# Attention in a one-core hybrid block: fp32r transposes of two probability row blocks, read from a DMA copy

## The chip, the cores and the metric

The kernel runs on one core of one Trainium2 chip. The metric is the device time of one execution in microseconds (us), as the median over several executions. A profile is one further execution taken by the hardware profiler; its trace tells when each instruction of each engine started and ended. The engines are TensorE (PE for matmuls, PEld for the loads of their weights), VectorE (DVE), ScalarE (ACT), GpSimd (POOL) and SyncE (SP), which issues nearly all DMAs here.

## The reference

One decoder block over 1024 tokens of width 1024, in float32. The part that matters is the forgetting attention, 8 heads of dimension 64, causal:

```python
logits = jnp.einsum('bqhd,bkhd->bhqk', qi, k).astype(jnp.float32) * scale
logits = logits + ci[..., None] - c_k          # c: running sum of the log forget gates
logits = jnp.where(causal, logits, -jnp.inf)
p = jax.nn.softmax(logits, axis=-1).astype(v.dtype)
return jnp.einsum('bhqk,bkhd->bqhd', p, v)
```

Beside it stand a gated MLP branch (GELU, a norm by groups, a 128x128 spatial mix), an output projection with residual, and a ConvFFN (up projection to 5632, causal depthwise convolution of width 3, SiLU gate, down projection), each behind an RMSNorm, and a final RMSNorm.

## The kernel before

**Numbers.** Most matmuls run in fp32r, a 4-byte type that TensorE streams faster than float32. A float32 operand is split in a high part rounded to fp32r and the rest, and a product is made of three matmuls. The transposes of the probabilities are float32.

**Stages.** Input projections (to about 205 us of the trace), the eight heads with the output projection of the gated branch as filler work (to about 358 us), the attention's output projection, the up projection with the convolution, and the down projection.

**One head.** Queries are cut in eight row blocks of 128, j = 0 to 7. Row block j sees the keys up to its own, 128(j+1) columns. Its steps are:
- `logits_mm` (L1002): the logits of block j on TensorE, in PSUM.
- `logits_min` (L1014): DVE adds the mask, takes the row minimum of the negated logits and writes them to SBUF. The blocks are kept in pairs i = j // 2 in tiles with the tags of `TTAG` (L954): pair 3 (blocks 6 and 7, 896 and 1024 columns) stands in `t3` for even heads and in a tile of the tag `H` for odd ones; pair 2 in `t2` and `H`. `places[h, i]` names the two parts.
- `logits_exp` (L1037): ACT takes the exponential in place, with the row sums beside it.
- `turn_p` (L1057): TensorE turns 128x128 blocks of probabilities with an identity (L1064), up to four into one PSUM bank. ACT copies the bank to fp32r (L1065) and DVE the rest (L1066). The block that is turned is the matmul's weights; the identity streams.
- `values` (L1071): TensorE multiplies by V and accumulates over the key blocks.

**The order of a head.** `GROUPS` (L1045) lists nine groups of key blocks. For the query blocks 4 to 7 (half 1) key blocks 0 to 4 are a group each and turn four blocks; ((1,5),(1,7)) turns blocks 5, 6, 7 and 7; ((1,6),(0,2)) turns 6, 7 and two of the lower half; the rest are of the lower half. `STEPS` takes them two by two: five steps (s = 0 to 4) a head. In step n the loop (L1186) turns the groups of step n+1, then multiplies those of step n with logits of the next head between them: `NEXT` (L1152) gives blocks 7 and 6 in step 0, 5 and 4 in step 1, and so on. The exponentials of a step's logits follow one step later. So blocks 7 and 6 of head h+1 have their logits in step 0 of head h, their exponentials in step 1, and are first turned in step 4. `FILLS` puts twelve filler matmuls (`sg_out`, L1092, with a load of `xtok` and a store to `hpd`) into steps 2 and 4 of heads 1 to 5 and into some more before; heads 6 and 7 have none. `seq` (L781) ties all matmuls of the heads on TensorE in one written order.

**Queues.** Instructions without such a tie are put in order on their engine when the program is built, by when their inputs are thought to be ready. SP holds, among others: the loads of a head's queries and keys two heads ahead (`head_loads`, L888), the load of the turned row sums (`row_tail`, L956, L964), the loads of the attention's output weights into the tag `raw` (`wo_load`, L1125, L1128), which POOL splits (L1136, L1137), and behind them, into the same four `raw` buffers, the first loads of the up projection's weights (L1273, L1326). ACT, DVE and POOL work on each other's outputs and wait on semaphores.

**The identity** is made by POOL in float32 (L135, L136). It is also used for the turns of the gated branch (L843), the row sums (L961), the next stage's input (L1390) and two small ones (L512, L628).

**Tags** (`BUFS`, L97): `H` has four buffers of 8 KB a partition. They hold parts of the input and its combinations early on (L195, L196, L398), then the odd heads' row blocks and `attF`, the heads' outputs.

Of the kernel before, what the change touches and what calls it, by code (L numbers as in the profile page):

```python
# [8 lines left out]
F32 = mybir.dt.float32  # L9
F32R = mybir.dt.float32r  # L10
# [4 lines left out]
P = 128  # L15
# [59 lines left out]
def block_kernel(ctx: ExitStack, tc: tile.TileContext, xT, xtok, wuv, wuh, wv0, wva, wvk, wvl, wqk, cpk, bfv,  # L75
                 ggain, g2r, gfr, wsp, woa, wos, wup, wdn, out):
    nc = tc.nc
# [15 lines left out]
    def nm(s):  # L93
        uid[0] += 1
        return f"{s}_{uid[0]}"

    BUFS = {"x1": 4, "x2": 2, "t3": 1, "t2": 1, "t01": 1, "V": 4, "H": 4, "wy": 2, "gg": 2,  # L97
            "pt": 3, "G": 4, "A": 2, "whl": 4, "raw": 4}

    LATE = ("A", "G", "whl", "pt")  # L100
# [1 line left out]
    def sb(tag, shape, dt=F32):  # L102
        return (base if tag == "x1" else raws if tag == "raw" else late if tag in LATE else early).tile(shape, dt, tag=tag, bufs=BUFS[tag], name=nm(tag))

# [3 lines left out]
    def fbank():  # L108
        return psa.tile([P, 512], F32, tag=FTAG, bufs=FB, name=nm("pf"))
# [22 lines left out]
        pe.matmul(wps, warm[:, 0:P], warm, start=True, stop=True)  # L132
    dve.memset(one, 1.0)
    dve.memset(lim, BIG)
    ident = cst.tile([P, P], F32, name="ident")  # L135
    make_identity(nc, ident)  # L136
    maskb = cst.tile([P, P], BF16, name="maskb")
    pool.memset(maskb, 0.0)
    pool.affine_select(out=maskb, in_=maskb, pattern=[[-1, P]], compare_op=ALU.is_ge,
# [44 lines left out]
    def xset(tags):  # L184
        r = []
        for t in tags:
            if t == "x1":
                r.append([sb(t, [P, 2, 512], F32R) for _ in range(2)])
            else:
                b = sb(t, [P, 2, 2, 512], F32R)  # L190
                r.append([b[:, 0], b[:, 1]])
        return r

    RAW = {n: [sb(t, [P, 2, 512]) for t in tags] for n, tags in (
        ("x21", ("V", "V")), ("x11", ("H", "H")), ("x22", ("x1", "x2")), ("x12", ("t3", "t2")))}  # L195
    XS = {n: xset(tags) for n, tags in (("B11", ("V", "V")), ("T2", ("H", "H")), ("B21", ("x1", "x2")))}  # L196

    def xs(n, hl, k):
        return XS[n][k // 2][hl][:, k % 2, :]
# [581 lines left out]
    def seq(m):  # L781

        if order:
            after(tc, m, order[0])
        order[:] = [m]
# [165 lines left out]
    attF = [None] * 4  # L951


    TTAG = [("gg", "gg"), ("wy", "wy"), ("t2", "H"), ("t3", "H")]  # L954
    exs = []
    def row_tail(h):  # L956

        p, hh, rs = h // 2, h % 2, rows[h]
# [55 lines left out]
    def logits_min(h, j, ps):  # L1014

        i, jj = j // 2, j % 2
        w1, w2 = (2 * i + 1) * P, (2 * i + 2) * P
        if jj == 1:
            tp = sb(TTAG[i][h % 2], [P, w1 + w2])
            places[h, i] = (tp[:, 0:w1], tp[:, w1:w1 + w2])  # L1020
        n = (j + 1) * P
        mn = sml.tile([P, 1], F32, tag="mn", name=nm("mn"))
        o, s, k = places[h, i][jj], ps[:, 0:n], msk[:, 1024 - n:1024]
        if chunk(n) < min(n, 512):
            o, k = (v.rearrange("p (b c) -> p b c", b=2) for v in (o, k))
            s = ps.rearrange("p (b c) -> p b c", b=2)[:, :, 0:chunk(n)]
        m = dve.tensor_tensor_reduce(out=o, in0=s, in1=k, scale=ss1[:, j:j + 1],
                                     scalar=lim[:, 0:1], op0=ALU.add, op1=ALU.min, accum_out=mn)
        if h and j == 5:
            after(tc, m, recips[h - 1])  # L1030
        if h and j == 3:
            after(tc, m, los[-1])
        if h == 7 and j == 0:
            after(tc, m, los[-2])
        return mn

    def logits_exp(h, j, mn):  # L1037
        t = places[h, j // 2][j % 2]
# [18 lines left out]
    def turn_p(g):  # L1057

        ptr = bank()
        pt = sb("pt", [P, 2, 512], F32R)  # L1060
        for half, k, j0, c, w in spans(g):
            for j in range(j0, 4 * half + 4):
                o = c + (j - j0) * P
                seq(pe.transpose(ptr[:, o:o + P], places[g[0], j // 2][j % 2][:, k * P:(k + 1) * P], ident))  # L1064
        casts.append(act.copy(pt[:, 0, :], ptr))  # L1065
        los.append(dve.tensor_tensor(out=pt[:, 1, :], in0=ptr, in1=f32(pt[:, 0, :]), op=ALU.subtract))  # L1066
        return pt
# [24 lines left out]
    def sg_out(whs):  # L1092
        for hf in range(2):
            o = slice(hf * 512, hf * 512 + 512)
            for tt in range(8):
                if hf == 0 and tt == 6:
                    nxt = sg_load(1)
                ts_ = slice(tt * P, (tt + 1) * P)
                hs = sb("raw", [P, 512])
                sp.dma_start(out=hs, in_=xtok[ts_, o])  # L1100
                ps = fbank()
                for k in range(4):
                    w = whs[k]
                    seq(pe.matmul(ps, sgT[k][:, 0, ts_], w[:, 0, :], start=(k == 0), stop=False))  # L1104
                    seq(pe.matmul(ps, sgT[k][:, 0, ts_], w[:, 1, :], start=False, stop=False))
                    seq(pe.matmul(ps, sgT[k][:, 1, ts_], w[:, 0, :], start=False, stop=(k == 3)))
                def evac(ps=ps, hs=hs, tt=tt, o=o):
                    dve.tensor_tensor(out=hs, in0=ps, in1=hs, op=ALU.add)
                    sp.dma_start(out=hpd[tt, :, o], in_=hs)

                if dve.on:
                    EVAC.append(evac)
                else:
                    evac()
                if hf == 0 and tt == 7:
                    whs = [None] * 4
                    SPLIT[:] = [(whs, k, nxt[k]) for k in range(4)]
                yield
# [67 lines left out]
    for n, step in enumerate(STEPS):  # L1186
        h, s = n // 5, n % 5
        if s == 0 and h < 6:
            head_loads(h + 2)
        if h == 7 and s == 0:  # L1190
            for _ in filler:
                pass
            wo_load((0, 1))
            wo_load((2, 3))
        if h in (2, 4, 6) and s == 4:
            for o in (slice(0, 512), slice(512, 1024)):
                pair_half(h // 2 - 1, o)
        now, turned = turned, []
        last, due = due, []
        if n == 35:  # L1200
            psl.release()
            psl = tc.alloc_tile_pool(name="psc", bufs=4, space=bass.MemoryType.PSUM, reuse_waits="tile")
            banks8[0, 0] = lbank()
            wmm(0, 0, banks8[0, 0], (0,))
        for g in STEPS[n + 1] if n + 1 < len(STEPS) else []:
            if n == 36 and turned:
                for e in held + [mrow]:
                    after(tc, logits_exp(*e), casts[-1])
            turned.append(turn_p(g))
            if n == 36 and len(turned) == 2:  # L1210
                after(tc, casts[-1], exs[-1])
        if n == 34:
            mrow = (7, 0, logits_min(7, 0, mrow))
        if n == 33:

            held, last = last, []
        if n == 34:
            last, held = held[:1], held[1:] + last
        if n == 35:
            last, held = held[:1], held[1:]  # L1220
        if s == 1 and h % 2 == 0:
            attF[h // 2] = sb("H", [P, 2, 1024])
        if s == (1 if h < 7 else 2):
            recips[h] = dve.reciprocal(rows[h], rows[h])
        out_copy = None
        if n == 37:
            row_tail(7)
        if n in EARLY:
            wmm(0, 0, banks8[0, 0], EARLY[n])
        if n == 39:  # L1230
            banks8[4, 0] = lbank()
            wmm(4, 0, banks8[4, 0], (0,))
        for c, (g, pt, js) in enumerate(zip(step, now, NEXT[s])):
            out_copy = values(g, pt) or out_copy
            last_copy = out_copy
            if h < 7:
                for j in js:
                    if n == 33 and j == 0:
                        mrow = logits_mm(7, 0, place())
                        continue  # L1240
                    due.append((h + 1, j, logits_min(h + 1, j, logits_mm(h + 1, j, place()))))
            if s == 1 and h < 7 and c == 0:
                row_tail(h)

        for e in last:
            x = logits_exp(*e)
            after(tc, x, casts[-1] if n == 34 else out_copy or casts[-1])
        fill((h, s))
        for _ in range(min(len(SPLIT), 1 if n == 9 else 2)):
            ws_, k, wr = SPLIT.pop(0)  # L1250
            wt = sb("whl", [P, 2, 512], F32R)
            ws_[k] = wt
            after(tc, act.copy(wt[:, 0], wr), out_copy or casts[-1])
            pool.tensor_tensor(out=wt[:, 1], in0=wr, in1=f32(wt[:, 0]), op=ALU.subtract)
        if n == 2:
            vh = sb("A", [P, 2, 4, 256])
            sp.dma_start(out=vh, in_=vu.rearrange("h p m c -> p h m c"))
        if n in UPPER:
            tt = UPPER.index(n)
            low = evac_v(tt, 1, vh[:, tt // 4, tt % 4, :])  # L1260
            after(tc, low(), los[-1])
            after(tc, vhigh[0], exs[-1])
# [631 lines left out]
```

## Time and profile before

| | before |
|---|---|
| median of 3 executions | 1045.37 us (1044.67 to 1045.62) |
| profiled execution | 1043.81 us, its span 1042.1 us |
| granted TensorE clock, mean | 0.998 of full |
| matmuls on PE | 4998 |
| transposes of probabilities (L1064) | 288 |
| bytes by DMA | 161.66 MB, 155 GB/s over the span |

The span runs from the first to the last instruction. A line of a view names source line, engine, operation and the tiles written and read, out<-in, with the buffer's tag (`t` for `t3`, `H`, `gg`, `wy`). A row of the stretches has the stretch and its length, then busy us and the number of instructions for PE, PEld, DVE, ACT and POOL, then the granted clock, the share of the 16 DMA engines and GB/s. On a timeline a row has start and length in us, the engine (with a q for its sequencer, which issues DMAs), the line and a count of merged instructions. Matmuls are pipelined, so the start of the next one, and not the length of one, tells what a matmul costs.

### The profile page before, as it was taken

The numbers are of one execution on the slowest core, as the hardware profiler recorded it, in microseconds if no ns is written. First come the engines' busy times: TensorE is split into PE (matmuls) and PEld (weight loads), VectorE is DVE, ScalarE is ACT, GpSimd is POOL, SyncE is SP. The second block draws the span as 40 slices with busy tenths as digits, with TensorE's granted clock in tenths as the row PEclk, the third lists the DMA queues.
The fourth block names the chain that finished last, engine by engine and source line by source line (L and its number), as shares of the span: only waits on it lengthen the run. The fifth ranks groups of instructions, "written<-read, shape, count | busy, mean of one in ns | idle before, by whom it ended". The sixth has DMA issues, their size and how long they took to land.

```text
span 1042.1 us, 14271 instructions
## 1 busy us (share of the span) xinstructions
PE 1034.4 (99%) x4998; PEld 869.6 (83%) x4998; DVE 892.3 (86%) x1302; ACT 564.2 (54%) x1003; POOL 221.9 (21%) x167
## 2 busy tenths in 40 slices
PE   9999999999999999999999999999999999999997
PEld 7988888988888888888888888888888888888886
DVE  6899887888888888998999998898997857997774
ACT  6776632457776857644444444444544544444654
POOL 0000232500322540343334323333331000000000
PEclk9999999999999999999999999999999999999999
DMA  9622558885645553231353432332322998333432
GB/s 340 231 82 97 153 156 250 238 256 171 203 130 172 187 169 111 81 122 60 131 178 131 139 120 71 132 101 81 122 81 91 327 330 293 110 92 101 150 115 99
DMA packets 67467, 161.66 MB, mean 155 GB/s; under 512 B 8110, under 2 KB 9254, under 8 KB 67396
## 3 DMA queue, kind: packets, MB, share of 16 engines
q1 hardware_dynamic: 67124, 160.72, 47.6%
q8 instruction: 39, 0.64, 0.3%
q14 instruction: 32, 0.26, 0.1%
q10 hardware_dynamic: 272, 0.04, 0.0%
HBM read 115.68 MB, written 45.05 MB: 154 GB/s over the span
## 4 chain that ended last, share of the span: by engine, by line
PE 98%; DVE 0%; DMA 0%; ACT 0%; SPq 0%; issue 0%; DVEq 0%
PE pb L1440 23%; PE pk L1440 17%; PE pb L1704 11%; PE pk L1704 9%; PE ps L283 5%; PE pb L283 5%; PE pk L1145 4%; PE pb L1080 3%; PE pb L1064 3%; PE qc L522 2%; PE qd L522 2%; PE qa L522 2%; PE pl L1010 2%; PE ps L873 2%; PE pl L1011 2%; PE pf L1104 1%
## 5 line engine op out<-in xcount | busy, mean ns | idle before, releaser
L1440 PE MATMUL pb<-xT,whb 128*128 128x512 f32 x804 | 189.4, 389 | 0.0
L1440 PEld LDWEIGHTS pb<-xT,whb 128*128 128x128 f32 x804 | 150.9, 188 | 31.4
L1440 PE MATMUL pk<-xB,x 128*128 128x512 f32 x528 | 127.2, 390 | 0.0
L1704 PE MATMUL pb<-whb,x 128*128 128x512 f32 (+1 forms) x528 | 119.2, 387 | 0.0
L1440 PEld LDWEIGHTS pk<-xB,x 128*128 128x128 f32 x528 | 98.8, 188 | 20.8 <-DVE x L172 0.4
L1704 PEld LDWEIGHTS pb<-whb,x 128*128 128x128 f32 x528 | 98.3, 188 | 20.3 <-DVE x L172 0.2
L166 ACT CAST x<-sg 128x512 fp32r<-128x512 f32 x77 | 47.8, 622 | 96.8 <-PE pk L1704 46.1
L166 ACT CAST whb<-sg 128x512 fp32r<-128x512 f32 x82 | 50.5, 617 | 83.9 <-PE pb L1440 83.0
L1704 PE MATMUL pk<-whb,x 128*128 128x512 f32 (+1 forms) x408 | 91.8, 386 | 0.0
L1704 PEld LDWEIGHTS pk<-whb,x 128*128 128x128 f32 x408 | 75.9, 188 | 15.5
L172 DVE TENSOR_TENSOR x<-sg,x 128x512 fp32r<-128x512 f32 x77 | 52.7, 687 | 39.4 <-ACT x L166 39.3
L1490 DVE SCALAR_TENSOR_TENSOR ca<-h,cp,ca 128x1023 f32<-128x1023 f32 (+1 forms) x44 | 67.9, 1544 | 3.9 <-ACT ca L1489 3.9
L1490 DVE SCALAR_TENSOR_TENSOR cg<-h,cp,cg 128x1023 f32<-128x1023 f32 (+1 forms) x44 | 65.5, 1489 | 5.5 <-ACT cg L1489 5.2
L1440 PE MATMUL pb<-xB,whb 128*128 128x512 f32 x264 | 63.8, 389 | 0.0
L1440 PE MATMUL pk<-xT,whb 128*128 128x512 f32 x252 | 61.0, 389 | 0.0
L172 DVE TENSOR_TENSOR whb<-sg,whb 128x512 fp32r<-128x512 f32 x82 | 57.1, 697 | 4.4 <-ACT whb L166 4.3
L1065 ACT CAST pt<-pb 128x512 fp32r<-128x512 f32 x72 | 40.4, 584 | 37.1 <-PE pb L1064 24.4
L1440 PEld LDWEIGHTS pb<-xB,whb 128*128 128x128 f32 x264 | 49.5, 188 | 10.7 <-issue 0.4
L1337 POOL TENSOR_TENSOR sg<-raw 128x512 f32<-128x512 f32 x20 | 30.2, 1511 | 131.1 <-DVE whb L172 74.5
L1066 DVE TENSOR_TENSOR pt<-pb,pt 128x512 fp32r<-128x512 f32 x72 | 47.4, 686 | 10.8 <-ACT pt L1065 10.1
L1440 PEld LDWEIGHTS pk<-xT,whb 128*128 128x128 f32 x252 | 47.2, 188 | 10.0 <-DVE whb L172 0.3
L1080 PE MATMUL pb<-pt,V 128*128 128x512 f32 (+3 forms) x192 | 49.0, 360 | 0.1
(414 smaller groups left out, 2154.1 us busy)
## 6 DMA issues: line engine op xcount, KB each, us to landing
raw<-wup SPq DMA_DIRECT2D x44, 512.0 KB
sg<-hx SPq DMA_DIRECT2D x77, 256.0 KB
hx<-hs SPq DMA_DIRECT2D x44, 256.0 KB
hx<-ca SPq DMA_DIRECT2D x35, 256.0 KB
xT<-wdn SPq DMA_DIRECT2D x28, 256.0 KB
x<-kd SPq DMA_DIRECT2D x24, 256.0 KB
A<-xtok SPq DMA_DIRECT2D x8, 512.0 KB
raw<-wqk SPq DMA_DIRECT2D x8, 512.0 KB
```

The lines of the kernel that those rows point to most:

```text
L166: cast[:] = [act.copy(h, src)]
L172: return eng.tensor_tensor(out=l, in0=src, in1=f32(h), op=ALU.subtract)
L283: pe.matmul(banks[m], xs(n, xi, k)[:, ms], w[:, wi, :], start=(first and k == 0 and c == 0 and (own or m % 2 == 0)), stop=(k == 3 and c == ...
L522: pe.matmul(ps, w[:, wi, ks], xs(n, xi, k), start=(first and c == 0), stop=(c == 11), skip_group_check=True)
L1064: seq(pe.transpose(ptr[:, o:o + P], places[g[0], j // 2][j % 2][:, k * P:(k + 1) * P], ident))
L1065: casts.append(act.copy(pt[:, 0, :], ptr))
L1066: los.append(dve.tensor_tensor(out=pt[:, 1, :], in0=ptr, in1=f32(pt[:, 0, :]), op=ALU.subtract))
L1080: seq(pe.matmul(po[half][:, o:o + w], lhs, pt[:, s, c:c + w], start=(new and s == 0), stop=(s == 1 and (half, k) in ((1, 6), (0, 3))), ski ...
L1145: seq(pe.matmul(ps, attT[k][:, a, ts_], w[:, b, :], start=(k == 0 and n == 0), stop=(k == 3 and n == 2)))
L1440: pe.matmul(ps, w[:, wi, ks], xb[:, xi, k, :], start=(first and n == 0), stop=(n == 11), skip_group_check=True)
L1490: return [dve.scalar_tensor_tensor(out=c[:, n:1024], in0=h[:, 0:1024 - n], scalar=w[2 - n], in1=c[:, n:1024], op0=ALU.mult, op1=ALU.add) f ...
L1704: pe.matmul((banks[bk + m] if ps is None else ps)[:, o], xh[:, xi, ms], wh[:, wi, o], start=((first and p_ == 0 or new) and n == 0), stop= ...
```

## The change

For heads 1 to 7 the pair 3 (row blocks 6 and 7) is copied within SBUF by two DMAs from its place to a tile of a new tag `C3`, and turned from there. The copy and the identity are read as fp32r for these transposes, 15 of the 36 in a head, 105 of 288 in all; head 0 stands in `C3` itself and is turned in float32 as before, as are all other blocks. The copies of head h+1 are issued on SP in step 2 of head h, after that step's turns in the program. The identity is made in a scratch tile and copied by ACT to fp32r; other uses read the same bits as float32. The tag `H` has two buffers instead of four, and the other two become the tags `C2` and `C3`: the input's combination T2 stands there early on, pair 2 of odd heads in `C2`. Pair 3 of heads 1 to 7 has the single place `t3`. The list `due_copies` stays empty.

```diff
-    BUFS = {... "V": 4, "H": 4, ...
+    BUFS = {... "V": 4, "H": 2, "C2": 1, "C3": 1, ...
...
-    ident = cst.tile([P, P], F32, name="ident")
-    make_identity(nc, ident)
+    identr = cst.tile([P, P], F32R, name="ident")
+    ident = identr.bitcast(F32)
+    id0 = sb("t01", [P, P])
+    make_identity(nc, id0)
+    act.copy(identr, id0)
...
-    XS = {n: xset(tags) for n, tags in (("B11", ("V", "V")), ("T2", ("H", "H")), ("B21", ("x1", "x2")))}
+    XS = {n: xset(tags) for n, tags in (("B11", ("V", "V")), ("T2", ("C2", "C3")), ("B21", ("x1", "x2")))}
...
-    TTAG = [("gg", "gg"), ("wy", "wy"), ("t2", "H"), ("t3", "H")]
-    exs = []
+    TTAG = (("gg", "gg"), ("wy", "wy"), ("t2", "C2"), ("t3", "t3"))
+    CTAG = (None, None, None, "C3")
+    exs, turns, due_copies = [], {}, []
...
-            tp = sb(TTAG[i][h % 2], [P, w1 + w2])
+            tp = sb(CTAG[i] if h == 0 and CTAG[i] else TTAG[i][h % 2], [P, w1 + w2])
             places[h, i] = (tp[:, 0:w1], tp[:, w1:w1 + w2])
+            turns[h, i] = places[h, i]
...
+    def copy_p(h, i):
+
+        w1, w2 = (2 * i + 1) * P, (2 * i + 2) * P
+        tp = sb(CTAG[i], [P, w1 + w2])
+        turns[h, i] = (tp[:, 0:w1], tp[:, w1:w1 + w2])
+        for jj in (1, 0):
+            sp.dma_start(out=turns[h, i][jj], in_=places[h, i][jj])
...
-                seq(pe.transpose(ptr[:, o:o + P], places[g[0], j // 2][j % 2][:, k * P:(k + 1) * P], ident))
+                t, o_ = turns[g[0], j // 2][j % 2][:, k * P:(k + 1) * P], ptr[:, o:o + P]
+                if g[0] and CTAG[j // 2]:
+                    seq(pe.transpose(o_.bitcast(F32R), t.bitcast(F32R), identr))
+                else:
+                    seq(pe.transpose(o_, t, ident))
...
                 sp.dma_start(out=hs, in_=xtok[ts_, o])
+                while due_copies:
+                    copy_p(*due_copies.pop(0))
...
+        if s == 2 and h < 7:
+            copy_p(h + 1, 3)
```

More of the change, by code (lines that the diff above doesn't have):

```diff
@@ L95, in nm @@
         return f"{s}_{uid[0]}"
-    BUFS = {"x1": 4, "x2": 2, "t3": 1, "t2": 1, "t01": 1, "V": 4, "H": 4, "wy": 2, "gg": 2,
+    BUFS = {"x1": 4, "x2": 2, "t3": 1, "t2": 1, "t01": 1, "V": 4, "H": 2, "C2": 1, "C3": 1, "wy": 2, "gg": 2,
             "pt": 3, "G": 4, "A": 2, "whl": 4, "raw": 4}
```

## The prediction

> **What bounds the kernel now.** I read the page first, then the head stage by stretches, then the transposes (L1064) by tile, and last the DMA queue around the seventh head.
>
> ```profile
> span 1042.1 us, 14271 instructions
> PE 1034.4 (99%) x4998; PEld 869.6 (83%) x4998; DVE 892.3 (86%) x1302; ACT 564.2 (54%) x1003; POOL 221.9 (21%) x167
> PE 98%; DVE 0%; DMA 0%; ACT 0%; SPq 0%; issue 0%; DVEq 0%
> ```
>
> TensorE (PE) is busy for 99% of the span, and the chain that ended last runs through it for 98%. So a TensorE microsecond saved or idled anywhere comes out at the end. The stage that the change touches, the eight heads, is this stretch (length, then busy us and count of PE, PEld, DVE, ACT, POOL, the clock, DMA share, GB/s):
>
> ```profile
> 221.00:358.00 137.00, 136.82 (x828) 120.76 (x827) 115.84 (x233) 99.07 (x225) 38.56 (x38) 1.00 0.57 172
> ```
>
> PE is idle for 0.18 of 137 us. DVE, the next, has 21 us to spare. Here too TensorE is the bound, and DVE can follow a stage that is some 4 us shorter.
>
> **What a transpose costs, and what fp32r may save.** First the transposes and the one of the row sums (L961) by tile, then an fp32r weight load, a run of eight transposes in the chain, and two fp32r matmuls of 128 columns on PE's timeline (start, us):
>
> ```profile
> L1064 PEld LDWEIGHTS pb<-ident,t x104: 137/140/144, 221.9 to 341.7; 128*128 128x128 f32 x104
> L961 PEld LDWEIGHTS pb<-ident,rs x8: 82/83/84, 231.5 to 354.2; 128*8 128x8 f32 x8
> L1010 PEld LDWEIGHTS pl<-x,x x96: 186/188/192, 209.4 to 346.1; 128*128 128x128 f32 x96
> 348.96 0.87 PE pb L1064 x8
> 239.83 0.22 PE L1010 MATMUL pl<-x,x 128*128 128x128 f32 x1
> 239.89 0.28 PE L1011 MATMUL pl<-x,x 128*128 128x128 f32 x1
> 240.00 1.06 PE L1064 MATMUL pb<-ident,H 128*128 128x128 f32 x8
> ```
>
> A transpose takes 0.87/8 = 109 ns of TensorE. It loads the probability block as weights and streams the identity through. Loading 8 columns takes 83 ns, 128 take 140: 0.475 ns a column, so some 61 ns of the 140 are the load itself and 79 are latency. The load overlaps the matmul before, so it isn't the 109; the f32 identity's 128 columns are. An fp32r matmul streams 128 columns in 239.89 - 239.83 = 60 ns when its weights are there. When they aren't, the next starts 110 ns on (239.89 to 240.00). An fp32r load lasts 188 ns, less the same 79 that is 109. So an fp32r transpose takes either 61 ns, if its load stays like today's transposing load, or 109, if it becomes like every fp32r load of this trace. I take 61: the short load belongs to transposing, the short stream to the type. Bounds of the saving per block: 0 and 49 ns; taken 48.
>
> Per head 15 blocks change type: two in each of the groups of key blocks 0 to 4, three in the group of 5 and 7, two in that of 6. In three of the four steps the last transpose before the value matmuls is one of them. The next weights there are fp32r (109 ns), and they can't load before that transpose starts, so it saves nothing. 12 x 48 = 0.58 us a head, 3.5 us for heads 1 to 6. Head 7 gives 0 to 0.6; I take 0, as the chain runs through ACT and DVE there. Sum: -3.5, between 0 and -4.1 (if the three count too: -5.2).
>
> **The copies.** Each head adds two DMAs in SBUF, 512 and 448 KB (0.98 MB). They can start when the exponentials of rows 7 and 6 are written and the last head's blocks are turned, and must land before the next head's first turns, two steps on. For heads 1 to 7 that window is, from the end of the exponential of row 6 to the start of the first eight transposes:
>
> ```profile
> 234.07:240.00 5.93, 5.93 (x35) 5.19 (x34) 4.00 (x10) 3.72 (x9) 0.00 (x0) 1.00 0.60 185
> 252.13:258.17 6.04, 6.04 (x37) 5.30 (x35) 5.31 (x12) 4.62 (x11) 0.00 (x0) 1.00 0.14 47
> 270.29:276.33 6.04, 6.04 (x37) 5.26 (x35) 4.22 (x10) 4.35 (x11) 1.30 (x1) 1.00 0.39 140
> 288.46:294.48 6.02, 6.02 (x37) 5.31 (x35) 4.56 (x10) 3.82 (x9) 0.00 (x0) 1.00 0.17 46
> 306.60:312.64 6.04, 6.04 (x37) 5.26 (x35) 4.21 (x10) 3.83 (x10) 0.00 (x0) 1.00 0.16 46
> 324.76:330.79 6.03, 6.03 (x36) 5.25 (x35) 4.20 (x10) 3.82 (x9) 0.00 (x0) 1.00 0.16 54
> 342.93:346.48 3.55, 3.53 (x25) 3.06 (x23) 3.34 (x9) 3.52 (x8) 3.55 (x4) 1.00 0.76 294
> ```
>
> No copy within SBUF is in the trace. Its nearest rows are loads of 512 KB, two queued together and one alone:
>
> ```profile
> 342.80:346.30 3.50, 3.48 (x22) 3.02 (x21) 3.29 (x9) 3.48 (x10) 3.50 (x5) 1.00 0.81 300
> 349.06:350.00 0.94, 0.94 (x10) 0.90 (x8) 0.77 (x4) 0.92 (x2) 0.94 (x2) 1.00 0.00 0
> 350.00:352.40 2.40, 2.40 (x17) 2.05 (x16) 1.93 (x4) 2.22 (x8) 2.40 (x3) 1.00 0.77 218
> ```
>
> So 300 GB/s, 3.3 us for the pair (218 GB/s: 4.5), and about 1 us from issue to movement (the lone load is issued at 349.06, and until 350.0 nothing moves). Heads 2, 4, 5 and 6 have 6.0 us and some 50 GB/s of other traffic: they fit. Head 3 (140 GB/s) just fits. Head 1 has 1.10 + 0.98 MB against 300 x 5.93 = 1.78 MB, but a quarter MB of its own is queued behind: 0 to 1 us late; taken 0.
>
> The Trainium skill, "DMA: Bandwidth & Descriptors", section "Where 436 GB/s comes from", bounds transfers within SBUF by 435 GB/s. By it the pair takes an estimated 2.3 us, and each landing below comes 1.0 us earlier. No run so far shows it.
>
> Head 7 doesn't fit. No filler matmuls are left in head 6, the window is 3.55 us, and the queue already moves 294 GB/s. The rows are ACT's, PE's and SP's timelines and the queue's waits:
>
> ```profile
> 341.56 0.19 ACT L1039 ACTIVATION_READ_ACCUMULATOR H<-H,mn 128x1 f32 x1
> 341.92 0.27 ACTq L963 DMA_DIRECT2D rsd<-t  x1
> 342.75 0.18 ACT L1039 ACTIVATION_READ_ACCUMULATOR H<-H,mn 128x1 f32 x1
> 341.69 0.38 PE L1064 MATMUL pb<-ident,t 128*128 128x128 f32 x2
> 346.48 1.06 PE L1064 MATMUL pb<-ident,H 128*128 128x128 f32 x8
> 341.83 0.33 SPq L1128 DMA_DIRECT2D raw<-woa  x1
> 342.21 3.57 SPq L1273 DMA_DIRECT2D raw<-wup  x2
> 349.06 3.94 SPq L1326 DMA_DIRECT2D raw<-wup  x2
> 353.11 5.16 SPq L964 DMA_DIRECT2D H<-rsd  x2
> SPq L1326 <- POOL G L1137: 6.4, 2, 3.2
> SPq L964 <- DMA rsd<-t: 4.2, 1, 4.2
> ```
>
> SP takes its DMAs in an order fixed at build time, and not that of the program: the load of row sums (L964, head 6) stands behind four loads of `wup` that the program issues after the whole loop, though its data was stored at 341.92. So the order goes by when the build thought each ready. Those loads issue at 342.21, 345.45, 349.06 and 352.68 (of a row x2, the second issue is its last 0.33 us), the last three held until POOL frees their buffers. The copies of rows 7 and 6 become ready at 342.1 and 342.93, within a microsecond of that store, so I expect them near L964: behind the third or the fourth load, hence behind POOL. Behind the third: issued at 349.4 and 349.8, and 0.52 + 0.98 MB at 300 GB/s from 350.0 land at 355.0. TensorE wants the first copied block two transposes after 346.48, at 346.7. POOL's work starts from head 5's output, so savings of heads 1 to 5 move both; those of head 6 (0.6) move TensorE alone. Wait: 355.0 - 346.7 + 0.6 = 8.9 us. Everything on TensorE stands in one written order behind that transpose (values, logits, output projection), so nothing fills it. Behind the fourth, 3.6 us more: 12.6.
>
> An idle TensorE also loses its clock. The end of the kernel (last two columns before the DMA's: POOL and clock) and its eight warming matmuls:
>
> ```profile
> 1036.00:1038.75 2.75, 0.12 (x2) 0.00 (x0) 1.44 (x5) 1.82 (x5) 0.00 (x0) 1.00 0.50 191
> 1038.76:1042.10 3.34, 0.00 (x0) 0.00 (x0) 0.00 (x0) 0.00 (x0) 0.00 (x0) 0.50 0.38 157
> 1.29 3.48 PE L132 MATMUL ps<-gg 128*128 128x512 bf16 x8 [1.29 <-DVE pad L143]
> ```
>
> 2.6 us after the last matmul the granted clock is 0.50. The first eight take 3.48 us, some 3.2 of them at half rate: a long wait costs 1.6 us more.
>
> The Trainium skill, "TensorE: Matmul & The Clock Gate", section "What's actually happening", halves the clock after an idle window of about 3.4 us, not 2.6. By it a wait under 3.4 us costs no clock; longer ones cost an estimated 1.7 us.
>
> **What costs nothing.** The identity gains one ACT copy before ACT's first product:
>
> ```profile
> 1.19 0.29 POOL masks.py:199 TENSOR_SCALAR_AFFINE_SELECT ident<-ident 128x128 f32<-128x128 f32 x1
> 3.27 0.51 ACT L55 ACTIVATE V<-H,g 128x256 fp32r<-128x256 f32 x1 [0.52 <-DMA g<-cpk]
> ```
>
> The identity is ready at 1.48, and ACT idles 0.52 us before 3.27; half of a 256-column step fits. Without that cover, 0.3 us. The 14 issues take SP 0.33 us each, and behind them stand row sums, stores and the next head's loads, needed a head later. The renamed tiles add no instruction; a row block's place is free once its copy has landed, which its turn needs anyway.
>
> **Sum.** -3.5 + 8.9 + 1.6 = +7.0 us. The profiled execution took 1043.81 us (span 1042.1 and 1.7 around it); on that, 1050.8. It lies 1.6 under the median of the runs, 1045.37, from which I predict: 1052.4. Behind the fourth load: -3.5 + 12.6 + 1.6 = +10.7, 1056.1.
>
> **The rivals.**
> In time: head 7's copies stand ahead of the loads and land by 346. For it: six of seven windows have room. Against: the exponential of row 6 ends at 342.93, after two loads have gone. It decides if both copies are issued by about 342. Price -3.5 to -4.1: 1041.9 to 1041.3.
> Little lost: they stand behind only the first `wup` load (landing at 342.8 + 2.03 MB / 300 = 349.6, wait 3.5, clock 0 to 1.6: 1045.4 to 1047.0) or the second (issued at 345.45, landing at 351.4, wait 5.3: 1048.8). For it: in program order they come first. Against: L964 does too.
> No faster: fp32r transposes are bound by a 109 ns load, so the change doesn't do what it says. The wait stays: 1055.9 or 1059.6. For it: every fp32r load here. Against: the transposing load is shorter.
>
> **How the numbers follow.** Forecast (third or fourth load) 0.53, in time 0.20, little lost 0.20, no faster 0.07. Likeliest: 1052.4; its own range is 1051 to 1056.5. The range 1041.5 to 1056.5 takes in the other sign and leaves out the no-faster case and gains over 3.9. A measurement of this kernel can tell about 0.2%, 2.1 us, from no change. Faster: 0.20. Same: half of little lost, 0.10. Slower: 0.70.
>
> **What would show it.** Right: 105 transposes as fp32r with 60 ns between starts and 140 ns loads; a gap on PE before the third transpose of head 7, released by a DMA, with the clock at 0.50 after it; the two copies behind `wup` loads on SP. Wrong: no gap there (then -3.5), 109 ns between them, or gaps in heads 1 to 6.

## The result and the profile after

| | before | after |
|---|---|---|
| median of 4 executions each | 1045.09 us (1044.67 to 1045.62) | 1057.78 us (1057.28 to 1059.79) |
| profiled execution, its span | 1043.81 us, 1042.1 us | 1057.86 us, 1056.1 us |
| granted TensorE clock, mean | 0.998 | 0.992 |
| bytes by DMA | 161.66 MB | 168.54 MB |

The ratio of the mean times is 1.0125, 95% interval 1.0107 to 1.0142. By the medians the change is slower by 12.7 us, where 7.0 was forecast; by the profiled executions by 14.05 us.

The page of the changed kernel, the same lines as before:

```profile
span 1056.1 us, 14298 instructions
PE 1035.7 (98%) x4998; PEld 869.9 (82%) x4998; DVE 892.5 (85%) x1302; ACT 564.0 (53%) x1004; POOL 221.3 (21%) x167
PE 95%; POOL 1%; DVE 1%; ACT 1%; DMA 1%; issue 1%; SPq 0%; DVEq 0%; POOLq 0%
```

TensorE has the same 4998 matmuls and is busy for 1035.7 us, against 1034.4. So of the 14.0 us by which the span grew, 1.3 are longer busy time and 12.7 are idle time. The chain's share on TensorE falls from 98% to 95%, and other links stand where it waited. It has one long wait through the heads, and two of 0.2 us:

```profile
PE pb L1080 <- DMA C<-t: 12.6, 1, 12.6
PE pb L966 <- DVE pt L1084: 0.2, 1, 0.2
PE pb L1082 <- DVE H L1107: 0.2, 1, 0.2
```

The first transpose of a copied block of head 7 (L1080, output `pb`) waited 12.6 us for the copy (`C<-t`). The stretches before, in and behind that wait (length, busy us and count of PE, PEld, DVE, ACT, POOL, clock, DMA share, GB/s):

```profile
221.00:346.00 125.00, 124.50 (x757) 108.80 (x755) 107.38 (x216) 90.33 (x205) 32.39 (x32) 1.00 0.72 221
346.19:358.77 12.58, 0.00 (x0) 0.00 (x0) 0.98 (x3) 0.00 (x0) 5.86 (x6) 0.68 0.83 224
358.77:364.30 5.53, 5.53 (x23) 5.04 (x24) 2.96 (x6) 3.05 (x6) 0.00 (x0) 0.50 0.02 8
364.30:368.00 3.70, 3.70 (x26) 3.15 (x25) 2.02 (x5) 3.22 (x10) 0.00 (x0) 1.00 0.00 0
```

Before the wait TensorE is nearly as full as before the change (0.50 us idle in 125). Behind it 5.53 us run at a clock of 0.50. SP's timeline shows the order that was forecast:

```profile
341.36 0.33 SPq L1148 DMA_DIRECT2D raw<-woa  x1
341.74 3.56 SPq L1295 DMA_DIRECT2D raw<-wup  x2
348.52 0.33 SPq L1348 DMA_DIRECT2D raw<-wup  x1
348.96 0.47 SPq L1049 DMA_DIRECT2D C<-t  x1
349.78 0.47 SPq L969 DMA_DIRECT2D H<-rsd  x1
350.32 1.08 SPq L1049 DMA_DIRECT2D C<-t  x1
352.08 0.34 SPq L1348 DMA_DIRECT2D raw<-wup  x1
```

The two copies (L1049) stand behind the third `wup` load (348.52), as forecast, with the load of head 6's row sums (L969) between them. The second copy was issued at 350.32, its last packet ended at 358.26, and TensorE went on at 358.77. (The second copy's rows are 3.5 KB, and no other packets there have that size, so its packets can be told from the rest.)

Against the trace of before, the same matmul began 0.70 us earlier when TensorE stopped, 12.05 us later when it went on, and 14.15 us later from the middle of head 7 to the end. So the sum of the profiled execution is -0.7 for the transposes of heads 1 to 6, +12.75 for the wait and +2.1 behind it.

The saving comes from runs like this, the first of head 4, in the changed kernel (L1082 f32 transposes, L1080 fp32r ones, L1098 the values) and in the kernel before (L1064, L1080 the values):

```profile
294.80 0.40 PE L1082 MATMUL pb<-ident,t 128*128 128x128 f32 x2
294.96 0.37 PE L1080 MATMUL pb<-ident,C 128*128 128x128 f32 x2
295.16 0.41 PE L1082 MATMUL pb<-ident,t 128*128 128x128 f32 x2
295.32 0.37 PE L1080 MATMUL pb<-ident,C 128*128 128x128 f32 x2
295.53 0.64 PE L1098 MATMUL pb<-pt,V 128*128 128x384 f32 x3
```

```profile
294.47 1.06 PE L1064 MATMUL pb<-ident,t 128*128 128x128 f32 x8
295.29 0.77 PE L1080 MATMUL pb<-pt,V 128*128 128x384 f32 x4
```

Start to start, the eight take 295.53 - 294.80 = 0.73 us, against 0.82: 0.09 saved, not 3 x 48 ns = 0.14 (of the four fp32r transposes, the last was not counted on). The length of each head, from its first transpose to the next head's, is worked out from such starts; three of the experiments below stand beside it:

| head | before | after | no copies | interleaved | xtok first |
|---|---|---|---|---|---|
| 1 | 18.17 | 18.18 | 17.93 | 18.04 | 17.93 |
| 2 | 18.16 | 18.45 | 17.81 | 18.33 | 17.96 |
| 3 | 18.15 | 18.16 | 18.18 | 18.15 | 18.15 |
| 4 | 18.16 | 17.79 | 17.79 | 17.66 | 17.79 |
| 5 | 18.16 | 17.80 | 17.80 | 17.66 | 17.80 |
| 6 | 15.69 | 15.39 | 15.39 | 15.24 | 15.38 |
| sum of differences | | -0.7 | -1.6 | -1.4 | -1.5 |

Heads 4 and 5 give 0.37 us, head 6 gives 0.30, head 2 loses 0.29, and heads 1 and 3 give nothing.

One caution for such tables: the 41st matmul began at 12.60 us before, at 12.61 after and up to 1.3 us later in the traces below, as the first loads land earlier or later. Whole spans of two single executions say little below 1 us; lengths of the same stretch say more.

### The profile page after: what moved, and what is told of

It is laid out like the page before. It is cut to its first block, busy times and chain, and to the rows that moved or that the text cites. A ratio compares the mean times of both kernels' runs of the same rounds, so it can differ in the third digit from the quotient of the medians.

```text
span 1056.1 us, 14298 instructions
## 1 busy us (share of the span) xinstructions
PE 1035.7 (98%) x4998; PEld 869.9 (82%) x4998; DVE 892.5 (85%) x1302; ACT 564.0 (53%) x1004; POOL 221.3 (21%) x167
## 2 busy tenths in 40 slices
DMA packets 69483, 168.54 MB, mean 160 GB/s; under 512 B 8334, under 2 KB 9478, under 8 KB 69412
## 4 chain that ended last, share of the span: by engine, by line
PE 95%; POOL 1%; DVE 1%; ACT 1%; DMA 1%; issue 1%; SPq 0%; DVEq 0%; POOLq 0%
PE pb L1462 23%; PE pk L1462 17%; PE pb L1726 11%; PE pk L1726 9%; PE pb L286 5%; PE ps L286 5%; PE pk L1165 4%; PE pb L1098 2%; PE qc L525 2%; PE qd L525 2%; PE qa L525 2%; PE ps L876 2%; PE pb L1082 1%; PE pl L1015 1%; PE pf L1124 1%; PE pf L1125 1%
## 5 line engine op out<-in xcount | busy, mean ns | idle before, releaser
L1098 PE MATMUL pb<-pt,V 128*128 128x512 f32 (+3 forms) x192 | 49.7, 364 | 0.1
```

Of the source, the lines that this page charges most:

```text
L1098: seq(pe.matmul(po[half][:, o:o + w], lhs, pt[:, s, c:c + w], start=(new and s == 0), stop=(s == 1 and (half, k) in ((1, 6), (0, 3))), ski ...
```

## The experiments

Each is set beside the kernel before, run on the same chip. Source lines of the experiments are shifted by a few against the changed kernel's.

**Head 7 left out** (`e1_heads_1_to_6`).

```diff
-        if s == 2 and h < 7:
+        if s == 2 and h < 6:
             copy_p(h + 1, 3)
...
-                if g[0] and CTAG[j // 2]:
+                if 0 < g[0] < 7 and CTAG[j // 2]:
```

> Heads 1 to 6 keep the copies and the fp32r transposes; head 7 is turned as f32 from its place, with no copies. Theory (the loss is head 7's wait alone; the other heads' transposes save a little): no wait of TensorE on a DMA, clock 1.00 through the stage, and what the trace of the changed kernel had gained when the gap began, 0.7 us: 1044.4 us (1043.4 to 1044.9). Rival A (the sum of the prediction was right in its first term): 3.5 us below before, 1041.6. Rival B (copies or fp32r transposes cost in every head): above 1047.

Measured: 1044.47 us against 1044.76, ratio 0.9996 (0.9987 to 1.0005). Through head 7 the stretch is full and the clock stays:

```profile
346.20:368.00 21.80, 21.74 (x123) 18.59 (x122) 17.17 (x29) 14.18 (x30) 9.57 (x9) 1.00 0.57 197
```

The whole loss hangs on head 7. The other heads' saving is the 0.7 us of the table, and too small to be told from no change by medians. Both rivals fall.

**The fourth `wup` load held back** (`e7_fourth_load_after`). My first theory for the long transfer was that the copies shared the DMA engines with the load issued behind them.

```diff
-        sp.dma_start(out=wr, in_=wup[i, :, 0:2, :])
+        d = sp.dma_start(out=wr, in_=wup[i, :, 0:2, :])
+        if i == 1:
+            waits(tc, d, copied[7])
```

> All of the change; the fourth wup load waits until the last copy of head 7 has landed. Queue position of the copies unchanged (behind the third load). Theory (the copies shared the queue's 300 GB/s with the fourth load, 0.5 MB, that was issued behind them): the last landing comes 0.52 MB / 245 to 300 GB/s = 1.7 to 2.1 us earlier, the wait falls from 12.6 to 10.5 to 10.9 us, total 1055.7 to 1056.1. Rival (transfers are served in order of issue and the copies themselves are slow here): wait 12.6 us still, 1057.8.

Measured: 1057.81 us, ratio 1.0128 (1.0114 to 1.0142). The wait, and the DMA engines' stretches during it:

```profile
PE pb L1080 <- DMA C<-t: 12.0, 1, 12.0
```

```profile
350.00:353.00 3.00, 0.00 (x0) 0.00 (x0) 0.00 (x0) 0.00 (x0) 2.52 (x3) 0.55 0.90 217
353.00:356.00 3.00, 0.00 (x0) 0.00 (x0) 0.00 (x0) 0.00 (x0) 0.00 (x0) 0.50 0.97 299
356.00:358.50 2.50, 0.00 (x0) 0.00 (x0) 0.00 (x0) 0.00 (x0) 0.00 (x0) 0.50 0.34 87
```

The theory falls: the wait is 0.6 us shorter, not 1.7 to 2.1, and the total is no better. But without the fourth load the last stretch shows something that it had covered: from 356.0 to 358.5 the engines are busy 0.34 of the time and move 87 GB/s, while hardly more than the end of the second copy is under way. So it seems that a few of the 16 engines finish late. What could have loaded them unevenly is the row-sum load between the copies, which has 64 rows and not 128.

**The row sums behind the copies** (`e9_row_sums_after`).

```diff
-        sp.dma_start(out=attF[p][hh * 64:hh * 64 + 64, 1, :], ...)
+        def ld(): return sp.dma_start(out=attF[p][hh * 64:hh * 64 + 64, 1, :], ...)
+        if h == 6: held_ld.append(ld)
+        else: ld()
...
             copy_p(h + 1, 3)
+            if h == 6:
+                after(tc, held_ld.pop()(), copied[7])
```

> All of the change; the load of head 6's row sums (64 rows of 4 KB) is ordered behind the two copies of head 7 instead of between them. The copies still stand behind the third wup load. In the run before this one, with the fourth wup load held back, the wait was still 12.0 us, so the fourth load is not the cause. Theory (some of the 16 DMA engines carried the row sums' rows between the two copies, and the last copy ended with the slowest of them): the last landing comes 1 to 2.5 us earlier, wait 10 to 11.5 us, total 1055.3 to 1056.8. Rival (the third load's slow start and the copies themselves take the time): wait 12 to 12.6 us, 1057.3 to 1058.

Measured: 1056.05 us against 1044.45, ratio 1.0112 (1.0096 to 1.0127). The queue and the wait:

```profile
348.50 0.33 SPq L1355 DMA_DIRECT2D raw<-wup  x1
348.94 1.30 SPq L1054 DMA_DIRECT2D C<-t  x2
350.30 1.46 SPq L970 DMA_DIRECT2D H<-rsd  x1
```

```profile
PE pb L1085 <- DMA C<-t: 10.1, 1, 10.1
```

TensorE goes on at 356.33 instead of 358.77. The second copy was issued 0.5 us earlier (349.77), so some 1.9 us are the transfer's. So the load of a quarter MB between the copies cost 2.4 us, as the theory said. Its reason, that the load was uneven among the engines, is read from the DMA share and not shown engine by engine.

**The copies ahead of the `wup` loads** (`e2_copies_first`).

```diff
             after(tc, d, loads[7])
+            after(tc, d, copied[7])
...
-        sp.dma_start(out=wr, in_=wup[i, :, 0:2, :])
+        d = sp.dma_start(out=wr, in_=wup[i, :, 0:2, :])
+        if i < AHEAD:
+            after(tc, d, copied[7])
```

> All of the change, but the first four wup loads are ordered behind the two copies of head 7 on SP's queue. Theory (the queue position is the cause): copies issued at about 342.2 and 343.1, landing some 4 us after the first issue as in heads 2 to 6, so 346.3 to 347.5 with the last woa load beside them; TensorE waits 0 to 1.3 us, clock stays 1.00: 1044 to 1046 us. If POOL's splits of the delayed wup loads come out late, a wait on POOL after head 7, up to 2 us more. Rival (the copies are slow in this stretch because of all the other traffic, wherever they stand): a wait of 5 us or more, 1050 or above.

Measured: 1045.60 us against 1044.76, ratio 1.0010 (1.0001 to 1.0019). SP's timeline, TensorE's wait, and the stretches ahead of, in and behind it:

```profile
341.94 0.33 SPq L1148 DMA_DIRECT2D raw<-woa  x1
342.37 1.12 SPq L1049 DMA_DIRECT2D C<-t  x2
343.59 1.34 SPq L1295 DMA_DIRECT2D raw<-wup  x1
```

```profile
PE pb L1080 <- DMA C<-t: 1.7, 1, 1.7
```

```profile
345.00:347.00 2.00, 1.67 (x11) 1.14 (x9) 1.93 (x6) 1.55 (x4) 2.00 (x4) 1.00 1.01 414
346.77:348.46 1.69, 0.00 (x0) 0.00 (x1) 0.98 (x3) 0.00 (x0) 1.69 (x2) 1.00 0.86 324
348.75:352.00 3.25, 3.25 (x13) 2.85 (x13) 2.19 (x5) 2.46 (x5) 3.25 (x5) 0.50 1.01 262
352.25:356.00 3.75, 3.75 (x26) 3.19 (x25) 2.11 (x4) 3.21 (x10) 0.43 (x1) 1.00 0.77 274
```

The place in SP's queue is the cause: 11 of the 12.6 us go with it, and no wait on POOL came in their place. Two things weren't expected. TensorE still waited 1.7 us, with the last `woa` load issued 0.4 us ahead of the copies; whether that load is the reason is the next experiment. And the clock, which I expected to stay, fell to 0.50 after only 1.7 us of idle time.

**Nothing ahead of the copies** (`e10_copies_and_woa`).

```diff
-            after(tc, sp.dma_start(out=wr, in_=woa[k]), loads[6])
+            d = sp.dma_start(out=wr, in_=woa[k])
+            after(tc, d, loads[6])
+            if k == 3:
+                after(tc, d, copied[7])
```

> All of the change, with the last woa load and the first four wup loads ordered behind the two copies of head 7, so that nothing stands ahead of the copies or moves beside them. Theory (1.7 us of wait were left in the run with the wup loads alone behind, because the last woa load went first): copies land by about 345.5 to 346.3, no wait, clock 1.00; heads 1 to 6 give 0.7 us and head 7 about 0.3: 1043.7 to 1044.2. Rival (the delayed loads make POOL and the output projection late): a wait on POOL of 1 us or more behind head 7, above 1045.

Measured: 1043.64 us against 1044.45, ratio 0.9994 (0.9985 to 1.0003). No wait on a DMA is left, the clock is 1.00 through head 7, and no wait on POOL came in its place:

```profile
346.00:368.00 22.00, 21.81 (x123) 18.61 (x124) 17.34 (x30) 14.94 (x32) 9.89 (x11) 1.00 0.70 242
```

The theory holds. The gain of 0.8 us is too small for the medians to tell from no change.

**The clock by itself** (`e8_clock_held`).

```diff
         pt = sb("pt", [P, 2, 512], F32R)
+        for _ in range(46 if g == (7, GROUPS[0]) else 0):
+            seq(pe.matmul(ptr, identr, V[0][:, 0, 0:4, :, :].rearrange("p h s d -> p (h s d)"), start=True, stop=True))
```

> All of the change, with 46 added fp32r matmuls of 512 columns (about 10.4 us, result overwritten) ahead of head 7's first transposes, where TensorE stood idle 12.6 us; the copies still land when they land. Theory (about 2 us of the loss is the clock that falls in the idle time): clock stays at 1.00 after the wait, what is left of the gap is about 2 us, total 1055.5 to 1056.1. Rival (after the wait the loss comes from ACT and DVE starting again, not from the clock): 1057.8.

Measured: 1057.45 us, ratio 1.0123 (1.0110 to 1.0137); the profiled execution took 1056.61, against 1057.86. The stretches in and behind what is left of the wait:

```profile
358.34:359.82 1.48, 0.00 (x1) 0.00 (x1) 0.00 (x0) 0.00 (x0) 0.00 (x0) 1.00 0.88 337
359.82:365.00 5.18, 5.12 (x36) 4.42 (x37) 3.63 (x8) 4.73 (x11) 0.00 (x0) 1.00 0.03 13
```

After 1.48 us of idle time the clock stays at 1.00, and 5.18 us hold 36 matmuls, where 5.53 us held 23 in the changed kernel. From head 7's first fp32r transpose to the matmul that began at 355.98 before, the traces have 9.26 us before, 11.44 after, 9.13 here. So the clock is worth 2.1 to 2.3 us, and the rival, ACT and DVE starting again, nothing. The profiled total is higher than expected because this execution lost 0.9 us between 13 and 232 us, ahead of the edit, for a reason that stays open. The medians alone would not decide: 1057.45 lies nearer to the rival.

**The transposes without copies** (`e4_exp_as_fp32r`). The logits and probabilities of blocks 6 and 7 are rounded to fp32r in place.

```diff
-        m = dve.tensor_tensor_reduce(out=o, in0=s, ...
+        m = dve.tensor_tensor_reduce(out=o.bitcast(F32R) if h and j > 5 else o, in0=s, ...
...
-        exs.append(act.activation(t, t, AF.Exp, ...
+        o = t.bitcast(F32R) if h and j > 5 else t
+        exs.append(act.activation(o, t, AF.Exp, ...
...
-        if s == 2 and h < 7:
-            copy_p(h + 1, 3)
```

Pair 3 then needs two places in turn, `C3` and `t3`.

> No copies: the logits and the exponentials of rows 6 and 7 of heads 1 to 7 are written in place as fp32r (rounded, which changes the values), and the same 105 transposes are fp32r. This leaves the transposes' saving alone. Theory (the transposes themselves save about 0.36 us a head, and part is given back where TensorE runs into DVE, not because of the copies): 0.7 us for heads 1 to 6 and 0.3 for head 7, 1043.6 to 1044.1. Rival A (the copies' traffic caused the small waits in heads 2 and 4): the full 0.36 x 7 = 2.5 us, 1042.3. Rival B (48 ns a transpose as predicted): 4 us, 1040.8.

Measured: 1043.05 us against 1044.45, ratio 0.9985 (0.9976 to 0.9994). Between the theory and rival A: heads 1 and 2 give 0.24 and 0.35 where the changed kernel lost 0.01 and 0.29, so the copies cost 0.9 us there; head 3 gives nothing without copies either. Rival B falls.

What holds head 3 is in the traces. At one logits matmul, first before, then after, TensorE's weight load waits for DVE's row minimum:

```profile
288.46 0.19 PEld L1010 LDWEIGHTS pl<-x,x 128*128 128x128 f32 x1 [0.17 <-DVE mn L1027]
288.77 0.19 PEld L1015 LDWEIGHTS pl<-x,x 128*128 128x128 f32 x1 [0.50 <-DVE mn L1033]
```

DVE has no idle time in the 5.8 us around it, before or after (this is after):

```profile
283.70:289.50 5.80, 5.74 (x38) 4.85 (x37) 5.80 (x13) 4.48 (x10) 0.00 (x0) 1.00 0.71 217
```

Up to there TensorE had gained 0.36 us on head 3 of the kernel before, and this one wait takes all of it back, with copies and, by the same wait of 0.50 us, without.

**The `xtok` load ahead of the copies** (`e12_xtok_first`). The traces of before and after show what the copies did in heads 1 and 2: the load of `xtok` for a filler step and DVE's evacuation of its PSUM bank (`raw<-pf`), first before, then after, then in this experiment.

```profile
247.17 0.98 SPq L1100 DMA_DIRECT2D raw<-xtok  x2
...
256.58 0.69 DVE L1108 TENSOR_TENSOR raw<-pf,raw 128x512 f32<-128x512 f32 x1 [0.37 <-PE pf L1106]
```

```profile
250.96 1.41 SPq L1049 DMA_DIRECT2D C<-t  x2
253.07 1.49 SPq L1118 DMA_DIRECT2D raw<-xtok  x2
...
259.36 0.69 DVE L1128 TENSOR_TENSOR raw<-pf,raw 128x512 f32<-128x512 f32 x1
```

```profile
248.82 0.43 SPq L1119 DMA_DIRECT2D raw<-xtok  x1
251.65 0.50 SPq L1049 DMA_DIRECT2D C<-t  x1
...
257.05 0.69 DVE L1129 TENSOR_TENSOR raw<-pf,raw 128x512 f32<-128x512 f32 x1 [0.30 <-PE pf L1127]
```

The copies pushed the load 5.9 us back, and the evacuation 2.8 us, which holds one of the four PSUM banks in rotation that the transposes need too. In the changed kernel the next filler's weight load waits for that evacuation:

```profile
260.10 0.19 PEld L1124 LDWEIGHTS pf<-whl,G 128*128 128x128 f32 x1 [0.18 <-DVE raw L1128]
```

The edit, on top of the run with nothing ahead of the copies:

```diff
-                sp.dma_start(out=hs, in_=xtok[ts_, o])
+                xt_load[:] = [sp.dma_start(out=hs, in_=xtok[ts_, o])]
...
             copied[h] = sp.dma_start(out=turns[h, i][jj], in_=places[h, i][jj])
+            after(tc, copied[h], xt_load[0])
```

with `copy_p` called behind the step's filler.

> As the run with the last woa load and the first four wup loads behind the copies of head 7, and besides, the copies of every head are ordered behind the xtok load that the filler matmuls need (it stood behind the copies, and in head 2 moved from 247.2 to 253.1 us, whereupon the step's result was taken out of its PSUM bank at 259.4 instead of 256.6). Theory (this is why heads 2 and 3 gave nothing: one PSUM bank fewer): the stretch from 258 to 276 us falls from 18.45 to about 17.8 us and the one before it from 18.17 to 17.9, as in the run without copies; total 0.9 us under that run, 1042.7. Rival (the copies' traffic itself slows DVE or TensorE there): lengths stay at 18.45 and 18.17, 1043.6.

Measured: 1043.01 us against 1044.71, ratio 0.9986 (0.9977 to 0.9995). Head 1 takes 17.93 and head 2 17.96, as the theory said within 0.2 us, where the rival would have left 18.17 and 18.45; the 0.2-us wait for `H` is gone.

**The order 6, 4, 7, 5** (`e5_interleaved_six`, heads 1 to 6; `e11_woa_interleaved` and `e13_xtok_interleaved`, all seven heads, on top of the two versions above).

```diff
-            for j in range(j0, 4 * half + 4):
+            for j in sorted(range(j0, 4 * half + 4), key=((6, 4, 7, 5) if half else (0, 1, 2, 3)).index):
```

> Heads 1 to 6 with copies, head 7 as f32, and the four transposes of a key block issued in the order 6, 4, 7, 5, so that each fp32r one stands between f32 ones. Theory (an fp32r transpose's weights need about 85 ns, hidden only behind an f32 matmul's 109): an fp32r transpose then takes 60 ns wherever an f32 one follows; a run of eight transposes takes 875 - 4 x 49 = 680 ns instead of 777; gross another 0.4 us a head. If TensorE is still free to use it: 1042.1; if DVE and the PSUM banks hold it back: 1044. Rival (the 60 and 85 ns belong to the position in the run, not to the neighbour): runs stay at 777 ns, 1044.4.

> As the run with the last woa load and the first four wup loads behind the copies of head 7 (all seven heads with copies), and the transposes of a key block in the order 6, 4, 7, 5. Theory (both gains add): that run's 0.75 us plus 0.13 us a head, measured in heads 5 and 6 of the interleaved run: 1.6 us under before, 1042.9. Rival (the interleaving makes head 7's first fp32r transpose earlier by one place, and it waits for the copy): no better than without it, 1043.7.

> Both: xtok loads ahead of the copies, head 7's copies ahead of the woa and wup loads, and the order 6, 4, 7, 5. If all gains add: 0.75 + 0.9 + 0.9 = 2.5 us under before, 1041.9. Rival (DVE, busy 0.85 of this stretch, holds TensorE back before that): 1042.7.

Measured: 1043.85 against 1044.45, 0.9993 (0.9985 to 1.0002); 1043.46 against 1044.71, 0.9986 (0.9977 to 0.9995); 1042.62 against 1044.71, 0.9981 (0.9972 to 0.9989). The first three runs of eight in heads 4 and 5 take 0.61 to 0.67 us, start to start, where they took 0.68 to 0.73, and the heads fall from 17.80 to 17.66. So an fp32r transpose does cost less between f32 ones, but 0.13 us a head and not 0.4. With all seven heads the order gives 1043.46, between the theory's 1042.9 and the rival's 1043.7. In the last version all gains together would have given 1041.9; 1042.62 is near the rival's 1042.7, by which DVE holds TensorE back, but a new wait has a part in it too. It stands at 277.8, where TensorE waits 1.07 us before head 3's first fp32r transpose, now the first of its run. The profile names DVE's row minimum, but that ended at 277.80, and the transpose's weight load had begun at 277.78. The semaphore that the weight load's sequencer waited for just before was set by the copy (L1049), at 277.68, 0.7 us after the copy's last packet. So this wait is the copy's. The median is still the lowest measured, 0.19% under the kernel before.

## Why the prediction was wrong

**Right.** TensorE as the bound; the copies behind the third `wup` load; heads 1 to 6 without a wait on a copy; the one wait in head 7, with nothing on TensorE to fill it; the clock at 0.50 behind it. The sign and the mechanism stand; the sizes of the terms failed. That the measured time lies near the 1056.1 of copies behind the fourth load is chance, as they stood behind the third. (One small sum is off: 8.9 + 3.6 is 12.5 and not 12.6. Nothing hangs on it.)

**The wait, 12.75 us instead of 8.9.** The step that failed is "0.52 + 0.98 MB at 300 GB/s from 350.0 land at 355.0". The copies' last packet ended at 358.3, 3.3 us later, and 0.5 us more passed until TensorE's start, which the sum put at nothing. The bytes left out L969's 0.26 MB, although the prediction put the copies near that load. With the row sums behind them, the last packet ended at 355.4 and TensorE went on at 356.33 and not at 358.77. So the load between the copies is 2.9 of the 3.3 us, though TensorE's start moved by 2.4 alone. The other 0.4 us is transfer: 1.50 MB in 5.4 us, 277 GB/s, so 300 was nearly right for this crowded queue. Counted at 300 GB/s, the 0.26 MB would have added 0.9 us. Why they cost more stays open; uneven engines are likely and not shown. Alone, the copies are much faster: with hardly any other traffic the engines moved 372 GB/s in this stretch of head 1 of the changed kernel,

```profile
252.25:254.75 2.50, 2.50 (x14) 2.23 (x13) 2.50 (x6) 2.50 (x6) 0.00 (x0) 1.00 1.03 372
```

and 414 from 345 to 347 us with the copies first. The Trainium skill, "DMA: Bandwidth & Descriptors", section "Where 436 GB/s comes from", gives 435 GB/s within SBUF: near what copies alone reached here, and no guide to the landing of a copy queued among loads.

**The saving, 0.7 us instead of 3.5.** Three steps failed. "I take 61" was too low: 0.37 us a head, over 12 transposes that count, is 31 ns saved on each and not 48, between the bounds of 0 and 49. The order 6, 4, 7, 5 gives 0.50, so a part depends on the neighbour. Next, "behind them stand row sums, stores and the next head's loads, needed a head later" missed the `xtok` loads, needed a step later; ordered ahead, they give back 0.7 us in heads 1 and 2. And "DVE can follow a stage that is some 4 us shorter" took the 21 us to spare for an even reserve. In head 3 DVE has none: TensorE's weight load waits for its row minimum, 0.17 us before and 0.50 after. Head 3 gave nothing in any version but the last one, where TensorE had just waited 1.07 us and the head took 17.79.

**The clock, 2.1 us instead of 1.6.** The estimate went by the eight warming matmuls; here 5.53 us ran at half rate.

**Head 7's transposes, taken at 0.** Without a wait, head 7's length falls by 0.13 to 0.17 us: nearly right.

## What to carry to other kernels

A new DMA is costed at its place in the queue: what is held ahead of it, what lies between its parts, and every load that it pushes back, down to the one that frees a PSUM bank. A stage average of spare DVE or DMA time says nothing about the step where the load lands, or where TensorE next needs DVE's result. And when a wait is removed by moving a transfer forward, look at the last load still ahead of it: here one of 0.5 MB cost 1.7 us and the clock with it.

## What the runs showed of the hardware that I had not expected

- The granted clock fell after 1.7 us of idle TensorE (0.50 from 348.7 to 352.1, 3.4 us) and did not after 1.48 us. In the changed kernel it fell 4.5 us after TensorE stopped (346.2 to 350.65) and came back at 364.30, 5.5 us after TensorE went on. The Trainium skill, "TensorE: Matmul & The Clock Gate", section "What's actually happening", has a free-running window of about 3.4 us. The 3.4 us at half rate agree; that a whole idle window is needed doesn't, since 1.7 us did.
- A load of 64 rows of 4 KB between two copies of 128 rows delayed TensorE by 2.4 us, more than their 0.26 MB take at the 217 to 299 GB/s of that queue (0.9 to 1.2 us).
- An fp32r transpose took less time between f32 transposes than in pairs: runs of eight, with four or five of them, took 0.61 to 0.67 us, against 0.68 to 0.73, with the same load of about 141 ns.
